# The modulation vector's sum: DVE's multiply-adds replaced by ACT's scaling and an adding transfer

## The chip, the cores and the metric

The kernel runs on one core of one Trainium2 chip. The metric is the device time of one execution in microseconds: the median of three runs is 1697.87 us (1697.62 to 1698.13). TensorE does the matrix products, ACT (ScalarE) and DVE (VectorE) the elementwise work, GpSimd (POOL) little beside issuing some transfers, and SP issues nearly all loads. All transfers run on 16 DMA engines.

## The reference

Two transformer layers, one after the other, on x of 1 x 256 x 2048 in float32. The first is a norm, a mix of three kinds of attention, a projection, and a wide layer of squared-ReLU units, then a norm. The second one is modulated by a vector c of 2048 numbers. Only this part matters here:

```
mod = silu(c) @ w_ada + b_ada                 # w_ada: 2048 x 6144
shift, scale, gate = split(mod, 3)
h = rmsnorm(x, pre_g) * (1 + scale) + shift   # then the second layer's products with h
...
return x + gate * rmsnorm(o, post_g)
```

silu(c) @ w_ada is a product of one row with 48 MiB of weights.

## The kernel before

Weights are float32 and are multiplied as a high and a low part. A *chunk* is one load of weights, mostly 1 MiB (128 partitions x 2048 columns) into one of four `raw` buffers (pool `rawp`, `NRAW = 4`). Its two halves of 1024 columns are split one by one: ACT writes the high part (L402), DVE subtracts it from the raw half to get the low part (L403). The parts go to one of six pairs of split tiles (`NSPLIT = 6`), and TensorE multiplies them with the activations (L265, L266 for products with features on the partitions; L297 to L299 for those with tokens).

`run` (L360) walks over the chunks in program order. For each half chunk it issues the loads up to four chunks ahead (`do_dma`), the splits up to four halves ahead (`do_split`), and the half's products; then `pump` (L345) lets each of the side generators take one step. A generator that yields n skips n steps. `drain` (L350) runs a generator to its end at once. After the first eight half chunks the order of instructions on each engine is set by a scheduler, which goes by program order as priority and by its own estimate of when operands are there, and which hands out the buffers of a pool; on the chip each engine then works through its queue in order, and SP and GpSimd do so with the transfers that they issue.

The modulation is such a generator, `ada_gen` (L1033). It is spawned after the first four half chunks of the wide layer. For each of three thirds (shift, scale, gate) it goes through 16 row blocks k: it loads 128 rows x 2048 columns of `w_ada` (1 MiB) into a buffer `rawa` of the same pool of four (L1042), and DVE adds it, times silu(c) of the row on each partition, to the accumulator `acc` (L1044 for the first block, L1046 for the others). Each block yields 3, so there is one in four half chunks. After 16 blocks `acc` is cut into high and low parts (L503, L504), and TensorE sums over the partitions (L1090).

The wide layer has eight slices of 16 half chunks with `w_mlp_in` and 16 with `w_mlp_out`. Before the last 16 half chunks with `w_mlp_out`, `load_gf` (L1009) drains `ada_gen` and has GpSimd read the scale row `G` from DRAM and the gain `gf`; DVE multiplies with both after each of the last products (L982, L985). That is 237 steps of `ada_gen` after its first. The gate's sums are taken in the last of these chunks, and the second layer's input is put together after them (`h3_gen`, L1136).

Of the kernel before, what the change touches and what calls it, by code (L numbers as in the profile page):

```python
# [13 lines left out]
ALU = mybir.AluOpType  # L14
# [16 lines left out]
class Chunk:  # L31
    """One load of weights: raw f32 columns, cut into nh pieces of high and low parts (hw columns each).
    Without a load, mm only uses what earlier chunks left. in_heap: the parts go to two general tiles each."""

# [9 lines left out]
class Joined:  # L44
    """Two tiles of 512 columns in place of one of 1024; a slice lies in one of them."""

# [10 lines left out]
def kernel(  # L57
# [23 lines left out]
    def table(name, after):  # L81
        """Switch the activation tables right after one of the engine's instructions."""
        with tc.issue_after(after.ins):
            return act.preload_act_table_set(name)
# [19 lines left out]
    def split_cols(dst, src, w=256):  # L104
        """dst[:, :w] and dst[:, w:2w] become the high and the low part of src."""
        act.activation(dst[:, 0:w], src, AF.Copy)
        ve.tensor_tensor(dst[:, w:2 * w], src, dst[:, 0:w], op=ALU.subtract)
# [3 lines left out]
    def rsqrt(dst, src, scale, tmp):  # L111
        """dst = (src * scale + EPS) ** -0.5 refined by one Newton step; tmp: two scratch views."""
        v, t = tmp
        ve.tensor_scalar(v, src, scale, EPS, op0=ALU.mult, op1=ALU.add)
        act.activation(dst, v, AF.Ln)
        act.activation(dst, dst, AF.Exp, scale=-0.5)
        ve.tensor_tensor(t, v, dst, op=ALU.mult)
        ve.tensor_tensor(t, t, dst, op=ALU.mult)
        ve.tensor_scalar(t, t, -0.5, 1.5, op0=ALU.mult, op1=ALU.add)
        return ve.tensor_tensor(dst, dst, t, op=ALU.mult)  # L120
# [3 lines left out]

# [1 line left out]
    wi = w_in[0].rearrange("(k p) n -> p k n", p=P)  # L126
# [16 lines left out]

    # the tensor engine's clock rises while it is busy: products that nothing reads, until the input is there
    def warm_up(n):
# [9 lines left out]

# [1 line left out]
    csq = H("csq")  # L157
# [47 lines left out]
    def setup_gen():  # L205
# [9 lines left out]
        yield 0  # L215
        # relative-position biases as vectors over distance, kept in DRAM for skewed reads
        for nh, c0, w, o_, bd in ((12, 0, 384, oh, bd1), (8, 12, 512, oh2, bd2)):
# [7 lines left out]
    def bias_tile(src, w, h0, hstep, joff, name):  # L225
        """[query, 2 heads, 256 keys] out of a per-distance vector."""
        b = H(name)
        base = src[:, :]
        po.dma_start(v2(b), bass.AP(tensor=base.tensor, offset=base.offset + h0 * w + joff,
                                    ap=[[1, P], [hstep * w, 2], [1, 256]]))  # L230
        return v2(b)[:, :, ::-1]

# [1 line left out]
    def W(ap):  # L234
        return ap.rearrange("(k p) n -> p k n", p=P)

    def modeA(src, c0, acts, evac, kt=KT, seg=None, need=None, name="a", k_row0=0, nh=2):
        """256 output features on partitions: psum [128, n, 512] = W.T @ [hi | lo]."""
        st = {}
# [37 lines left out]
    def modeB(dmas, acts, evac, ncols=512, kts=(4, 4, 4, 4), need=None, name="b", by_t=False):  # L277
        """tokens on partitions: psum [128, t, ncols] = act.T @ W. by_t: the first token block over the
        whole contraction, then the second; evac(ps, t) after each."""
        st = {"parts": {}}  # L280
# [149 lines left out]

# [1 line left out]
    h1 = [H(f"h1_{k}", F32R) for k in range(KT)]  # L432

    def x_transposes(src, dst, gain, name, kks):
        """dst[k] = split(gain * src.T) for the k-tiles kks (pairs)."""
        for k in kks:
# [15 lines left out]
    def sumsq(dst, src, name, scale=1.0):  # L452
        """dst [128,1] = sum of squares of scale * src [128, <=512]."""
        sc = H(f"sq_{name}")
        last["sq"] = act.activation(sc[:, 0:src.shape[-1]], src, AF.Square, scale=scale, accum_out=dst)

    def row_of(col, dst, name):
        """dst [128, 128]: every partition holds the token values of col [128, 1]."""
        pr = PA(f"pr_{name}")
        dg = H(f"dg_{name}")  # L460
        ve.tensor_scalar(dg[:, 0:128], ident, col, None, op0=ALU.mult)
        te.matmul(pr[:, 0:P], ones, dg[:, 0:128], start=True, stop=True)
        return ve.tensor_copy(dst, pr[:, 0:P])
# [22 lines left out]
    def evac_sum(ps, name, row=None):  # L486
        """[128, 2, 256] = the two halves of a feature-on-partition product, times a token row."""
        o = H(name)
# [11 lines left out]
    def in_parts(o, name):  # L500
        """o as high and low part."""
        hi, lo = H(f"{name}h", F32R), H(f"{name}l", F32R)
        act.activation(hi, o, AF.Copy)  # L503
        ve.tensor_tensor(lo, o, hi, op=ALU.subtract)  # L504
        return hi, lo
# [20 lines left out]

# [1 line left out]
    def ones_row_norm(tiles, width, name):  # L528
        """rstd row [128, 256] over the features of tiles ([128, 2, 256] each)."""
        parts = []  # L530
# [90 lines left out]

# [1 line left out]
    def softmax(segs, nsk, sk, n, name):  # L623
        """segs: [128, keys] logits, normalised in place; nsk, sk: [128, n] sink values, negated and plain."""
        nm, den, es = S(f"nm{name}", n), S(f"den{name}", n), S(f"es{name}", n)
# [14 lines left out]
    def swa_bias(h):  # L640
        """[query, keys of the second block, then of the first] for one head."""
        b = H("swab")
# [58 lines left out]

# [1 line left out]
    def gla_gen():  # L703
        QD, KI, OB = {}, {}, {}
        st = {}
        # gates
        pbl = PA("pbl")
# [193 lines left out]

# [1 line left out]
    wo = w_out[0]  # L903
    # contraction tiles: 0-5 sliding window (heads i and i+6), 6-9 stick-breaking, 10-15 gated
    def wo_dma(c0):
# [45 lines left out]

# [1 line left out]
    r2sq = C([P, 2], "r2sq")  # L953
# [65 lines left out]

    # modulation: silu(c) @ w_ada as multiply-adds, then one sum over partitions  # L1020
    wa = W(w_ada_2[0])
# [3 lines left out]
    gp = [None] * 4  # L1025
    # sel[:, n, m] = (n == m): sums over partitions, put into row n
    sel = C([P, 4, 4], "sel")
# [5 lines left out]
    def ada_gen():  # L1033
# [4 lines left out]
        for third in range(3):  # L1038
            acc = big.tile([P, D], F32, name="acc", tag="acc")
            for k in range(KT):  # L1040
                raw = rawp.tile([P, 2048], F32, name="rawa", tag="raw")
                sy.dma_start(raw, wa[:, k, third * D:(third + 1) * D])  # L1042
                if k == 0:
                    ve.tensor_scalar(acc, raw, e[:, 0:1], None, op0=ALU.mult)  # L1044
                else:
                    ve.scalar_tensor_tensor(out=acc, in0=raw, scalar=e[:, k:k + 1], in1=acc,  # L1046
                                            op0=ALU.mult, op1=ALU.add)
                yield 3
            parts = []
# [27 lines left out]
    def ada_row(r, third):  # L1077
        """(1 + scale) * pre_norm_g or gate * post_norm_g, into DRAM for reads by all partitions."""
        bg, pg_ = H("bada"), H("pada_g")
# [51 lines left out]

# [1 line left out]
    h3 = [H(f"h3_{k}", F32R) for k in range(KT)]  # L1133
    r3 = C([P, 2], "r3")

    def h3_gen(t):  # L1136
        for n in range(4):
            drain(recs["fin", n, t])
        u, r12 = S("u", 1), S("r12", 1)
        # (mean(y^2) / (mean(x^2) + EPS) + EPS) * (mean(x^2) + EPS), y = x * norm_final  # L1140
        ve.tensor_reduce(u, ss3[:, t, :], axis=AX.X, op=ALU.add)
# [26 lines left out]
    def make_xn():  # L1168
        with tc.issue_after(last["sum"].ins):
            # mean(x^2) + EPS out of the sum of squares scaled by EPS / D  # L1170
            ve.tensor_reduce(r3, ss3[:, :, 0:4], axis=AX.X, op=ALU.add)
# [31 lines left out]

# [1 line left out]
    def att_gen():  # L1205
# [118 lines left out]

    # grouped linear map of the pooling branch
    wpg = w_pool_group_2[0].rearrange("g (k p) d -> p (g k) d", p=P)
# [30 lines left out]

# [1 line left out]
    wm, wba, wbp = W(w_merge_2[0]), W(w_branch_attn_2[0]), W(w_branch_pool_2[0])  # L1359
# [37 lines left out]

# [1 line left out]
    wo2 = W(w_out_2[0])  # L1399
# [68 lines left out]
def _constants():  # L1468
    """Arrays that depend on shapes alone: identity, triangles, bucket one-hots, window counts."""
    import numpy as np  # L1470
# [56 lines left out]
```

## Time and profile before

| | |
|---|---|
| time, median of 3 runs | 1697.87 us (1697.62 to 1698.13) |
| profiled execution, from its first to its last instruction (span) | 1695.6 us |
| what lies around the span, against the median | 2.3 us |
| TensorE busy | 1681.5 us, 99% |
| DVE / ACT / GpSimd busy | 1154.3 / 860.6 / 56.7 us |
| DVE, multiply-adds of the modulation | 45 of 2349 ns |
| loads of the modulation | 48 of 1 MiB, first issued at 380.8 us, last at 967.8 us |
| transfers, whole span | 363.87 MB, mean 215 GB/s |

The profiled execution has no time of its own beside its span; the runs are timed without a profile. Busy times are shares of one engine's time; several engines work beside each other, so they do not add up to the span. The chain of waits follows the work back from the last instruction, and what lies on it set the end. A wait of an engine is its idle time before an instruction, put down to what came last.

### The profile page before, as it was taken

The page shows a single profiled execution, that of the slowest core. Times are in us where ns is not written, and L with a number is a line of the kernel's source. Part 1 is how long each engine was busy: PE and PEld are TensorE (multiplying, and loading weights), DVE is VectorE, ACT ScalarE, POOL GpSimd, SP SyncE. Part 2 cuts the span into 40 slices and gives each one's busy share as a digit, 9 for nine tenths or more (in the row PEclk, how much of TensorE's full clock was granted, in tenths as well). Part 3 has the DMA queues.
Part 4 walks back from the last instruction along what each step waited for, and adds up shares of the span by engine and source line. Part 5 has one row for each costly group of instructions (what it writes and reads, how often), then busy time and mean ns, then how long its engine had stood idle before and what let it go on. Part 6 is the DMA issues. An engine that isn't in the chain of part 4 may idle for free.

```text
span 1695.6 us, 23129 instructions
## 1 busy us (share of the span) xinstructions
PE 1681.5 (99%) x9085; PEld 1446.3 (85%) x9085; DVE 1154.3 (68%) x1437; ACT 860.6 (51%) x1278; POOL 56.7 (3%) x113
## 2 busy tenths in 40 slices
PE   9999999999999999999999999999999999999998
PEld 7888899888888888888888888788888888888887
DVE  6566767557787668777778775877775655555554
ACT  6455657445444444444444354665455544554442
POOL 2002100000000000000000010010100000000000
PEclk9999999999999999999999999999999999999999
DMA  9645646757888678877788876555645655565652
GB/s 322 190 138 139 153 140 172 199 188 264 283 296 280 219 246 292 281 282 238 277 279 288 285 245 214 172 188 180 194 156 167 215 184 189 184 188 185 214 188 71
DMA packets 265405, 363.87 MB, mean 215 GB/s; under 512 B 9809, under 2 KB 206063, under 8 KB 259152
## 3 DMA queue, kind: packets, MB, share of 16 engines
q1 hardware_dynamic: 261472, 353.53, 63.6%
q0 software_dynamic: 3792, 8.86, 2.6%
q8 instruction: 71, 1.16, 0.3%
q14 instruction: 38, 0.31, 0.1%
q10 hardware_dynamic: 32, 0.01, 0.0%
HBM read 360.20 MB, written 2.15 MB: 214 GB/s over the span
## 4 chain that ended last, share of the span: by engine, by line
PE 95%; DVE 2%; ACT 1%; DMA 1%; issue 0%; SPq 0%; DVEq 0%
PE ps_w L265 14%; PE ps_w L266 7%; PE ps_m L265 7%; PE ps_w L297 7%; PE ps_w L299 7%; PE ps_w L298 7%; PE ps_m L266 4%; PE ps_b L265 4%; PE ps_wo L299 3%; PE ps_wo L297 3%; PE ps_wo L298 3%; PE ps_b L266 2%; PE ps_gp L265 2%; PE ps_ga L265 2%; PE ps_u L265 2%; PE ps_q L265 2%
## 5 line engine op out<-in xcount | busy, mean ns | idle before, releaser
L402 ACT ACTIVATE hi<-raw 128x1024 fp32r<-128x1024 f32 (+3 forms) x570 | 588.1, 1034 | 733.4 <-PE ps_w L299 169.5
L403 DVE TENSOR_TENSOR lo<-raw,hi 128x1024 fp32r<-128x1024 f32 (+3 forms) x570 | 675.2, 1190 | 411.7 <-ACT hi L402 407.7
L265 PE MATMUL ps_w<-h,hi 128*128 128x512 f32 x1024 | 359.6, 397 | 0.0
L266 PE MATMUL ps_w<-h,lo 128*128 128x256 f32 x1024 | 286.1, 279 | 0.0
L265 PEld LDWEIGHTS ps_w<-h,hi 128*128 128x128 f32 x1024 | 192.2, 188 | 46.3
L297 PE MATMUL ps_w<-hi,sl 128*128 128x512 f32 x512 | 199.4, 389 | 0.0
L299 PE MATMUL ps_w<-hi,sl 128*128 128x512 f32 x512 | 199.3, 389 | 0.0
L298 PE MATMUL ps_w<-lo,sl 128*128 128x512 f32 x512 | 199.2, 389 | 0.0
L266 PEld LDWEIGHTS ps_w<-h,lo 128*128 128x128 f32 x1024 | 193.0, 188 | 0.3
L265 PE MATMUL ps_m<-h,hi 128*128 128x512 f32 x512 | 181.3, 399 | 0.0
L266 PE MATMUL ps_m<-h,lo 128*128 128x256 f32 x512 | 143.8, 281 | 0.0
L1046 DVE SCALAR_TENSOR_TENSOR acc<-rawa,silu_c,acc 128x2048 f32<-128x2048 f32 x45 | 105.7, 2349 | 30.3 <-DMA rawa<-in_w_ada_dram 30.1
L265 PEld LDWEIGHTS ps_m<-h,hi 128*128 128x128 f32 x512 | 96.2, 188 | 23.9
L299 PEld LDWEIGHTS ps_w<-hi,sl 128*128 128x128 f32 x512 | 96.1, 188 | 20.2
L297 PEld LDWEIGHTS ps_w<-hi,sl 128*128 128x128 f32 x512 | 96.1, 188 | 20.1
L298 PEld LDWEIGHTS ps_w<-lo,sl 128*128 128x128 f32 x512 | 96.1, 188 | 19.8
L266 PEld LDWEIGHTS ps_m<-h,lo 128*128 128x128 f32 x512 | 96.7, 189 | 0.0
L297 PE MATMUL ps_wo<-hi,mg 128*128 128x512 f32 (+1 forms) x160 | 55.5, 347 | 0.0
L299 PE MATMUL ps_wo<-hi,mg 128*128 128x512 f32 (+1 forms) x160 | 55.5, 347 | 0.0
L298 PE MATMUL ps_wo<-lo,mg 128*128 128x512 f32 (+1 forms) x160 | 55.5, 347 | 0.0
L995 DVE SCALAR_TENSOR_TENSOR xt<-ps_w,r2sq,xt 128x512 f32<-128x512 f32 x64 | 45.1, 745 | 8.1 <-PE ps_w L299 8.1
L265 PE MATMUL ps_b<-ya,hi 128*128 128x512 f32 x128 | 45.6, 399 | 0.0
(517 smaller groups left out, 2766.9 us busy)
## 6 DMA issues: line engine op xcount, KB each, us to landing
raw<-in_w_mlp_in_dram SPq DMA_DIRECT2D x64, 1024.0 KB, 5.6
raw<-in_w_mlp_out_dram SPq DMA_DIRECT2D x64, 1024.0 KB, 5.2
raw<-in_w_in_dram SPq DMA_DIRECT2D x48, 1024.0 KB, 5.0
rawa<-in_w_ada_dram SPq DMA_DIRECT2D x48, 1024.0 KB, 5.4
raw<-in_w_merge_dram SPq DMA_DIRECT2D x32, 1024.0 KB, 5.3
raw<-in_w_out_dram SPq DMA_DIRECT2D x20, 1024.0 KB, 5.1
raw<-in_w_in_dram SPq DMA_DIRECT2D x24, 768.0 KB, 4.5
raw<-in_w_in_dram SPq DMA_DIRECT2D x20, 512.0 KB, 5.2
```

Of the source, the lines that this page charges most:

```text
L265: te.matmul(ps[:, n, :], hi[:, s], a, start=(k == 0), stop=False)
L266: te.matmul(ps[:, n, 0:256], lo[:, s], a[:, 0:256], start=False, stop=(k == kt - 1))
L297: te.matmul(o, ah, hi[:, s], start=(k == 0), stop=False)
L298: te.matmul(o, ah, lo[:, s], start=False, stop=False)
L299: te.matmul(o, al, hi[:, s], start=False, stop=(k == ktot - 1))
L402: act.activation(hi[:, 0:c.hw], r, AF.Copy)
L403: ve.tensor_tensor(lo[:, 0:c.hw], r, hi[:, 0:c.hw], op=ALU.subtract)
L995: ve.scalar_tensor_tensor(out=d, in0=ps[:, t if isinstance(ts, tuple) else 0, :], scalar=r2sq[:, t:t + 1], in1=d, op0=ALU.mult, op1=ALU.add)
L1046: ve.scalar_tensor_tensor(out=acc, in0=raw, scalar=e[:, k:k + 1], in1=acc, op0=ALU.mult, op1=ALU.add)
```

## The change

In each block k, ACT now multiplies the two halves of the loaded buffer by silu(c), in two steps of the generator. In the first block of a third it writes to `acc`, in the others back into the buffer. Then, in the next step and except for the first block, a transfer that GpSimd issues adds the whole buffer to `acc` in place. DVE's instructions on L1044 and L1046 are gone. A block now takes a step for each half and one for the transfer, after which two are skipped. Comments and docstrings are gone as well.

```diff
             for k in range(KT):
                 raw = rawp.tile([P, 2048], F32, name="rawa", tag="raw")
                 sy.dma_start(raw, wa[:, k, third * D:(third + 1) * D])
-                if k == 0:
-                    ve.tensor_scalar(acc, raw, e[:, 0:1], None, op0=ALU.mult)
-                else:
-                    ve.scalar_tensor_tensor(out=acc, in0=raw, scalar=e[:, k:k + 1], in1=acc,
-                                            op0=ALU.mult, op1=ALU.add)
-                yield 3
+                dst = raw if k else acc
+                for i in range(2):
+                    half = slice(i * 1024, (i + 1) * 1024)
+                    act.activation(dst[:, half], raw[:, half], AF.Copy, scale=e[:, k:k + 1])
+                    yield 0
+                if k:
+                    po.dma_start(acc, raw, accum_op=ALU.add)
+                yield 2
             parts = []
```

## Rows read from the trace of the kernel before

**Rows 1.** Page: busy time of each engine (share, instructions), chain by engine.
```profile
PE 1681.5 (99%) x9085; PEld 1446.3 (85%) x9085; DVE 1154.3 (68%) x1437; ACT 860.6 (51%) x1278; POOL 56.7 (3%) x113
...
PE 95%; DVE 2%; ACT 1%; DMA 1%; issue 0%; SPq 0%; DVEq 0%
```

**Rows 2.** Windows: stretch and length, busy per engine, PEclk, DMA share, GB/s.
```profile
607.00:614.00 7.00, 7.00 (x40) 5.84 (x39) 4.26 (x6) 2.51 (x3) 0.00 (x0) 1.00 1.08 369
634.00:638.00 4.00, 4.00 (x25) 3.51 (x24) 3.96 (x6) 1.88 (x4) 0.00 (x0) 1.00 1.06 424
10.00:30.00 20.00, 18.81 (x111) 15.97 (x110) 14.67 (x25) 14.41 (x29) 3.79 (x14) 1.00 1.09 335
380.00:973.00 593.00, 593.00 (x3040) 503.05 (x3039) 454.34 (x442) 265.03 (x315) 4.03 (x8) 1.00 0.79 272
```

**Rows 3.** Waits of TensorE, whole span: total us, times, longest; the largest one.
```profile
PE pt_h L441 <- DMA xt<-in_x_dram: 1.8, 3, 0.9
```

**Rows 4.** Waits between 380 and 973 us, ACT's largest.
```profile
ACT hi L402 <- PE ps_w L265: 137.7, 86, 2.0
ACT hi L402 <- PE ps_w L299: 136.1, 85, 2.2
```

**Rows 5.** Waits of SP's queue between 380 and 973 us.
```profile
SPq L250 <- DVE lo L403: 148.1, 34, 5.6
...
SPq L250 <- DVE acc L1046: 52.5, 22, 2.4
SPq L1006 <- DVE acc L1046: 48.0, 21, 2.4
```

**Rows 6.** Instructions on rawa: ns min/median/max, first and last start; waits; landing.
```profile
L1042 SPq DMA_DIRECT2D rawa<-in_w_ada_dram x48: 340/341/341, 380.8 to 967.8; - x48
L1046 DVE SCALAR_TENSOR_TENSOR acc<-rawa,silu_c,acc x45: 2339/2351/2354, 399.4 to 972.7; 128x2048 f32<-128x2048 f32 x45
L1044 DVE TENSOR_SCALAR acc<-rawa,silu_c x3: 1281/1281/1281, 386.2 to 804.0; 128x2048 f32<-128x2048 f32 x3
...
  DMA rawa<-in_w_ada_dram: 30.1, 33
...
DMA to landing us min/median/max: 4.8/5.4/7.5
```

**Rows 7.** Groups by line, 380 to 973 us: count, busy us, mean ns, idle before.
```profile
L403 DVE TENSOR_TENSOR lo<-raw,hi 128x1024 fp32r<-128x1024 f32 x213 | 258.3, 1222 | 103.2 <-ACT hi L402 102.9
...
L402 ACT ACTIVATE hi<-raw 128x1024 fp32r<-128x1024 f32 x213 | 226.1, 1061 | 321.4 <-PE ps_w L265 137.7 <-PE ps_w L299 136.1 <-issue 40.1
```

**Rows 8.** Order of time, GpSimd: start, us, instruction.
```profile
1004.73 0.56 POOL L1014 DMA_DIRECT2D G<-gdr  x1
```

**Rows 9.** Page: DMA queues of SP and of GpSimd: packets, MB, share.
```profile
q1 hardware_dynamic: 261472, 353.53, 63.6%
q0 software_dynamic: 3792, 8.86, 2.6%
```

**Rows 10.** DMA issues by line: count, size of each, median us to landing.
```profile
raw<-in_w_mlp_in_dram SPq DMA_DIRECT2D x64, 1024.0 KB, 5.6
...
rawa<-in_w_ada_dram SPq DMA_DIRECT2D x48, 1024.0 KB, 5.4
...
G<-gdr POOLq DMA_DIRECT2D x4, 256.0 KB, 8.8
...
gp<-gdr POOLq DMA_DIRECT2D x4, 256.0 KB, 5.3
```

**Rows 11.** Order of time, SP: one modulation load's issue.
```profile
644.23 0.34 SPq L1042 DMA_DIRECT2D rawa<-in_w_ada_dram  x1
```

**Rows 12.** Order of time, DVE: the multiply-add of that load.
```profile
649.86 2.35 DVE L1046 SCALAR_TENSOR_TENSOR acc<-rawa,silu_c,acc 128x2048 f32<-128x2048 f32 x1 [0.59 <-DMA rawa<-in_w_ada_dram]
```

**Rows 13.** Order of time, DVE: the first products with gf and G.
```profile
1066.02 0.69 DVE L982 TENSOR_TENSOR xt<-xt,gf 128x512 f32<-128x512 f32 x1
1066.74 0.69 DVE L985 TENSOR_TENSOR Z<-xt,G 128x512 f32<-128x512 f32 x1
```

## The prediction

> **What bounds the kernel now.** I read the page first: TensorE is busy for 1681.5 of 1695.6 us, and the chain that ended last is 95% TensorE [rows 1]. Then the stretch in which the modulation runs, 380 to 973 us, in the view by windows: TensorE is busy in 593.00 of 593 us at the full granted clock (1.00), DVE in 454, ACT in 265, and the 16 DMA engines show a mean share of 0.79 at 272 GB/s [rows 2]. So nothing that DVE is relieved of can shorten this stretch; it can only stay or grow. The largest of TensorE's waits in the whole span is 1.8 us, for the input at the start [rows 3]: it never waits for weights here. What protects it is seen in the other waits: ACT's splits wait 137.7 + 136.1 us for TensorE to give a pair of split tiles back, so the splits run six half chunks ahead [rows 4]; and the load queue (SP) waits for a raw buffer to be given back, mostly by DVE's second half of the split, and for 48.0 and 52.5 us by the modulation's multiply-add [rows 5]. The four raw buffers are thus always claimed, with some spare time in each.
>
> **The pace.** The first modulation load starts at 380.8, the last of 48 at 967.8 us [rows 6]; by the code's counts they lie 209 half chunks of products apart (3 x 15 x 4 within the thirds, 17 and 12 between them), so a half takes 587.0 / 209 = 2.81 us. A piece is now due every 4 halves (11.2 us). In the new code a piece costs a step for the first half of the scaling, one for the second, one for the transfer and two skipped: 5 halves, 14.0 us.
>
> **Part by part.**
> 1. DVE loses 45 multiply-adds of 2349 ns and 3 first products of 1281 ns, 105.7 + 3.8 = 109.5 us [rows 6]. TensorE does not wait for DVE in this stretch, so it is worth 0.
> 2. ACT gains 96 activations of 128x1024. The nearest row is the split's first half, same tile shape, 1061 ns [rows 7]: 102 us in all, 2.1 per piece. ACT is busy 265/593 = 45% of the stretch, 6.3 of 14.0 us; with 2.1 more it has 5.6 us idle per piece. Hidden, as long as a scaling does not wait for its load by more than that; DVE's multiply-add waited 30.1 us over 33 cases [rows 6].
> 3. GpSimd gains 45 transfers. Issuing one takes it 0.56 us [rows 8], 25 us in all on an engine with 56.7 us of work [rows 1]: hidden.
> 4. The transfers themselves are the cost. They are 1 MiB each, tile to tile, with an add. The trace of before has no such transfer. Both queues are counted against the same 16 engines [rows 9], and GpSimd's four reads of G landed after a median of 8.8 us beside the weight stream, the same size of gp in 5.3 us with the stream thinner [rows 10]; so I let the new transfers share the engines with the loads. In 14.0 us these must bring 2.5 MiB of weights and 1 MiB of modulation. Rate of the loads: the longest dense stretch that I found beside the modulation gave 369 GB/s for 7 us, a short one 424 for 4 us, and the start 335 for 20 us [rows 2]. At 369 a MiB takes 1.0486 MB / 369 = 2.84 us, so 3.5 take 9.9 us and 4.1 are left. Lower bound of an add: it is charged as one pass over 1 MiB at the best rate, 2.47 us, and fits. Upper bound: it has to fetch both operands, 2 MiB, at 335 GB/s: 6.3 us. I take two operands at 424 GB/s, since its rows are 8 KB long in each partition as those of rawa: 4.9 us. Sum 9.95 + 4.95 = 14.9 against 14.0: 0.9 us over per piece, 36 us for the 40 transfers that are paced (6). With everything at 369 it is 15.6 (1.6 over), at 335 it is 17.2 (3.2 over).
> The Trainium skill has a rule on this price ("Collectives: The Full Stack", The bandwidth ceiling: the fold count and why AG ≠ RS ≠ AR): an add in the transfer engines issues two source reads, and the reduction ran at 32.35 GB/s where the plain copy ran at 62.28. By it the sum is that of two operands; no run here shows it yet.
> 5. Raw buffers. A piece holds its buffer from its issue at 644.23 to the end of the multiply-add at 652.21 us, 8.0 us [rows 11, 12]. Afterwards: landing 5.4 [rows 6], scaling 1.06, the next step 2.8 later, then the transfer, 5 to 11 us (one or two landings of 5.4): 14 to 21. A weight chunk needs at least 5.6 (landing) + 2.8 (the next half) + 1.06 + 1.22 (its split) = 10.7 us [rows 7, 10]. Per 14.0 us there are 4 x 14.0 = 56 buffer-us; 2.5 x 10.7 + 21 = 48. It fits until a transfer takes 19 us, but the spare time that hid late loads is mostly gone.
> 6. What is left over. The draining before the last eight output chunks comes 237 steps after the start. At 5 instead of 4 steps the modulation's last load would come at step 256 and its end at 264, so there 4 loads and 5 transfers are still to come: 40 of the 45 transfers are paced, 5 come in a heap. The heap is 4 x 2.84 + 5 x 4.9 = 36 us of transfer work, beside 8 MiB of weights (23 us), in 16 halves, 45 us: 14 us over. At 0 it would be spread into the gaps that the output products leave; at 36 nothing of it would be beside them. G, which GpSimd issued from 1004.7 us on with gf, DVE first used right after gf at 1066.0 [rows 8, 13]; both now stand behind these transfers on GpSimd's queue, which it works through in order. The cover is 61 us less a landing of 9; where the heap uses it up, the eight pairs of products with gf and G (0.69 + 0.69 us each) fall together at the end: up to 11 us more.
> Sum: 40 x 0.9 + 14 = 50 us over the stretch. The profiled execution spans 1695.6 us; the runs' median of 1697.87 is 2.3 more, which I leave as it is. 1697.9 + 50 = 1748 us. Time that TensorE has lost here does not come back, for it is the bound before and after it.
>
> **Rivals.**
> (a) The add is charged as one pass. Then 9.9 + 2.5 = 12.4 of 14.0 us, the heap is 4 x 2.84 + 5 x 2.47 + 23 = 47 of 45 us, and the time is 1698 to 1701, not slower. It is decided by whether a transfer takes under 4.1 us of the engines. For it: the mean of 272 GB/s leaves room below the 369. Against it: the room is there because no buffer was free (5), and this gets tighter.
> (b) The chain on the accumulator. Each transfer waits on GpSimd for the one before, since both change acc; behind it GpSimd has only the next ones, and the buffer it holds stops SP, which issues in order, so the weights wait too. It decides from 14.0 - 0.5 = 13.5 us per transfer on: at 18 us it costs 4.5 x 40 = 180, and with the heap 1892 us. For it: 256 KB of G took 8.8 us from GpSimd [rows 10], which times four is 35. Against it: two landings of 1 MiB are 10.8 us.
> (c) ACT becomes the late one. A scaling at the head of ACT's queue holds the splits behind it, and DVE behind these. If landings double to 10.8 us, a scaling waits some 5.4 + 2.1 = 7.5 us, 1.9 over ACT's idle 5.6: 40 x 1.9 = 76, and with the heap 1788 us. Against it: six half chunks of split weights, 16.9 us, stand between ACT and TensorE, so that a single late load is not felt.
> (d) Faster. TensorE's idle time outside the stretch is 1695.6 - 1681.5 = 14 us; a lucky new order around the second block's input at 1096 us could take a few of them: 1693. Nothing in the change aims there.
>
> **How the numbers follow.** My forecast with its own range of 1715 to 1800: 0.47. (a) 0.18, (b) 0.17, (c) 0.12, (d) 0.06. Below 0.2% (3.4 us) a measurement of this kernel can't tell a change. Faster is (d), 0.06; the same is (a), 0.18; slower is the rest, 0.76. The range takes in (a) and (c) and (b) up to a transfer of 17 us, 1695 to 1870.
>
> **What would show it.** TensorE's busy share in the modulation's stretch below 100%, with idle before products that waits put down to the splits, and these to loads or scalings that wait for rawa; DMA share near 1 there; acc transfers landing after 8 to 12 us; SP waiting on these transfers; the stretch longer by some 36 us, the rest between 1050 and 1130. Wrong, if TensorE is still full in it (then the add is cheap, (a)), if a transfer lands later than 13.5 us (b), or if the loss lies outside both stretches.

## The result and the profile after

The changed kernel takes 1854.28 us (median of 4 runs, 1850.64 to 1857.43) against 1697.89 us before: a ratio of 1.0921, interval 1.0907 to 1.0935. It is slower by 156 us, inside the range and on the side that was forecast, but three times the forecast loss of 50.

The page of the changed kernel: busy time of each engine, and the queues of SP (q1) and GpSimd (q0).
```profile
PE 1726.5 (93%) x9085; PEld 1469.7 (79%) x9085; DVE 1040.5 (56%) x1389; ACT 943.8 (51%) x1374; POOL 96.4 (5%) x158
...
q1 hardware_dynamic: 261472, 353.53, 57.6%
q0 software_dynamic: 10272, 56.05, 16.1%
```
Against [rows 1] the 9085 products take 45.0 us longer, and TensorE is idle for 1851.2 - 1726.5 = 124.7 us where it was for 14.1: 45.0 + 110.6 = 155.6 us, all of the loss. DVE's relief, 114 us, bought nothing.

Windows of the changed kernel (columns as in [rows 2]): from the first modulation load to where the kernel before had its last product with the MLP's first matrix (1008 us), from there to that product here (1095), and the output chunks behind it.
```profile
380.00:1008.00 628.00, 574.59 (x2836) 479.43 (x2836) 318.17 (x366) 303.18 (x363) 31.11 (x39) 0.96 0.91 273
1008.00:1095.00 87.00, 82.79 (x407) 69.24 (x406) 41.29 (x46) 42.56 (x50) 5.19 (x6) 0.96 0.94 282
1095.00:1235.00 140.00, 99.54 (x384) 77.39 (x384) 54.31 (x61) 52.60 (x62) 11.87 (x17) 0.85 0.93 269
```
TensorE was full at a granted clock of 1.00 in 593 of 593 us [rows 2]. Now it is idle for 53 us of the first stretch, 4 of the second and 40 of the third, and between such stalls it is granted 0.96 and 0.85 of its 2.4 GHz, in the mean. Parts of these stretches run at 1.2 GHz: some of the products with the MLP's first matrix take 796 ns where the median is 395. The engines of the DMA are busier, 0.91 to 0.94 in place of 0.79, yet they move no more: 273 GB/s in place of 272. The splits themselves take no longer beside the transfers: between 380 and 1008 us ACT's take 1.05 us and DVE's 1.22, against 1.06 and 1.22 [rows 7].

The products with the MLP's first matrix (ns min/median/max, first and last start):
```profile
L265 PE MATMUL ps_w<-h,hi x1024: 387/395/796, 383.9 to 1095.0; 128*128 128x512 f32 x171
```

DMA issues of the changed kernel: count, size, median us to landing.
```profile
raw<-in_w_mlp_in_dram SPq DMA_DIRECT2D x64, 1024.0 KB, 8.6
raw<-in_w_mlp_out_dram SPq DMA_DIRECT2D x64, 1024.0 KB, 7.8
...
rawa<-in_w_ada_dram SPq DMA_DIRECT2D x48, 1024.0 KB, 5.5
acc<-rawa POOLq DMA_DIRECT2D x45, 1024.0 KB, 8.2
```
The adding transfer lands after 8.2 us, the weights after 8.6 where it was 5.6 [rows 10]. The modulation's loads keep their 5.5: they start only when a transfer has ended, as the next two views show.

Waits of the changed kernel, whole span (total us, times, longest), first of the engines, then of SP's queue.
```profile
DVE lo L403 <- ACT hi L402: 649.9, 309, 22.1
...
ACT rawa L1046 <- DMA rawa<-in_w_ada_dram: 325.6, 43, 15.3
...
PE ps_w L297 <- ACT hi L402: 34.3, 10, 17.8
...
PE pt_z L1159 <- DVE Z L1156: 14.0, 1, 14.0
```
```profile
SPq L1042 <- DMA acc<-rawa: 199.3, 36, 13.5
...
SPq L1006 <- DMA acc<-rawa: 43.8, 4, 12.5
...
SPq L250 <- DMA acc<-rawa: 26.0, 4, 11.8
```
36 of the 48 modulation loads wait on SP for the transfer before them, since they were given its buffer; 269 us of SP's time goes this way, where DVE's multiply-add cost 100 [rows 5].

One such turn in order of time (start, us, engine).
```profile
487.07 0.34 SPq L1042 DMA_DIRECT2D rawa<-in_w_ada_dram  x1
...
493.50 2.19 ACT L1046 ACTIVATE rawa<-rawa,silu_c 128x1024 f32<-128x1024 f32 x2 [9.00 <-DMA rawa<-in_w_ada_dram]
...
495.98 0.86 POOL L1049 DMA_DIRECT2D acc<-rawa  x1 [16.16 <-ACT rawa L1046]
...
503.90 0.34 SPq L1042 DMA_DIRECT2D rawa<-in_w_ada_dram  x1
```
Load 6.4 us, scaling 2.5, transfer 7.9, and only then the next load: 16.8 us, where a piece is due every 14.0. That looked like the cause. By the engines' time it comes to the same: q1 takes 0.576 x 1851.2 us for 353.53 MB, 3.16 us of the 16 engines' time per MiB, and the transfers add (0.161 x 1851.2 - 0.026 x 1695.6) / 45 = 5.64 us each; 3.5 x 3.16 + 5.64 = 16.7 us per piece. The modulation's loads are in fact issued 16.8 us apart (the median). Two theories with one number: the experiments had to part them.

### The profile page after: what moved, and what is told of

Read it like the earlier page. It is cut to its first block, busy times and chain, and to the rows that moved or that the text cites. A ratio compares the mean times of both kernels' runs of the same rounds, so it can differ in the third digit from the quotient of the medians.

```text
span 1851.2 us, 23271 instructions
## 1 busy us (share of the span) xinstructions
PE 1726.5 (93%) x9085; PEld 1469.7 (79%) x9085; DVE 1040.5 (56%) x1389; ACT 943.8 (51%) x1374; POOL 96.4 (5%) x158
## 3 DMA queue, kind: packets, MB, share of 16 engines
q1 hardware_dynamic: 261472, 353.53, 57.6%
q0 software_dynamic: 10272, 56.05, 16.1%
## 5 line engine op out<-in xcount | busy, mean ns | idle before, releaser
L403 DVE TENSOR_TENSOR lo<-raw,hi 128x1024 fp32r<-128x1024 f32 (+3 forms) x570 | 668.1, 1189 | 653.5 <-ACT hi L402 649.9
L402 ACT ACTIVATE hi<-raw 128x1024 fp32r<-128x1024 f32 (+3 forms) x570 | 573.1, 1027 | 440.4 <-PE ps_wo L299 74.2
L265 PE MATMUL ps_w<-h,hi 128*128 128x512 f32 x1024 | 375.0, 409 | 36.6 <-DVE mlp L491 17.2
L266 PE MATMUL ps_w<-h,lo 128*128 128x256 f32 x1024 | 293.5, 287 | 5.0 <-DVE lo L403 5.0
L265 PEld LDWEIGHTS ps_w<-h,hi 128*128 128x128 f32 x1024 | 199.4, 195 | 88.1 <-ACT hi L402 22.5
L1046 ACT ACTIVATE rawa<-rawa,silu_c 128x1024 f32<-128x1024 f32 x90 | 99.3, 1143 | 325.6 <-DMA rawa<-in_w_ada_dram 325.6
L297 PE MATMUL ps_w<-hi,sl 128*128 128x512 f32 x512 | 206.9, 404 | 48.0 <-ACT hi L402 34.3
L266 PEld LDWEIGHTS ps_w<-h,lo 128*128 128x128 f32 x1024 | 200.3, 196 | 8.0 <-DVE lo L403 7.8
L299 PE MATMUL ps_w<-hi,sl 128*128 128x512 f32 x512 | 204.4, 399 | 0.0
L1049 POOL DMA_DIRECT2D acc<-rawa x45 | 39.2, 872 | 878.1 <-ACT rawa L1046 790.3
L265 PE MATMUL ps_u<-h,hi 128*128 128x512 f32 x128 | 45.6, 399 | 0.0
```

The costliest lines, as they stand in the source:

```text
L265: te.matmul(ps[:, n, :], hi[:, s], a, start=(k == 0), stop=False)
L266: te.matmul(ps[:, n, 0:256], lo[:, s], a[:, 0:256], start=False, stop=(k == kt - 1))
L297: te.matmul(o, ah, hi[:, s], start=(k == 0), stop=False)
L299: te.matmul(o, al, hi[:, s], start=False, stop=(k == ktot - 1))
L402: act.activation(hi[:, 0:c.hw], r, AF.Copy)
L403: ve.tensor_tensor(lo[:, 0:c.hw], r, hi[:, 0:c.hw], op=ALU.subtract)
```

## The experiments

LOOP: the buffer that goes load, scaling, transfer, load sets the pace. ENGINES: the transfer takes so much of the shared 16 engines that all loads land late, whoever waits for it. Diffs are against the changed kernel unless said; times are medians of 4 runs, beside 1698.0 to 1698.7 for the kernel before.

**e1_accacc.** acc is added to itself, so the scaled pieces are not summed; a buffer is free after its scaling.
```
- po.dma_start(acc, raw, accum_op=ALU.add)
+ po.dma_start(acc, acc, accum_op=ALU.add)
```


> The transfer adds acc to itself instead of the scaled piece (the sum is left out; bytes, add and chain on acc stay). A piece's buffer is free right after its scaling. LOOP (load 6.4 + scaling 2.5 + transfer 7.9 = 16.8 us run one after the other, since the next piece's load takes the buffer that the transfer holds): the loop falls to 9 us, SP no longer waits for transfers, the loss goes to under 40 us: 1700 to 1735 us, granted clock at least 0.99. ENGINES (loads are late since the 16 engines are full): the same bytes, so most of the loss stays: 1800 to 1855 us, weights land at a median of 8 us or more and ACT waits for them.


1826.63 us, 1.0757 (1.0741 to 1.0773). Not a clean test: with nothing to hold them the transfers ran ahead, back to back, some 11.4 us apart, and were through at 1129 us in place of 1205. e5 repeats it at pace.

**e2_plain.** The same order of instructions, the transfer a copy: the addition is left out.
```
- po.dma_start(acc, raw, accum_op=ALU.add)
+ po.dma_start(acc, raw)
```


> The transfer copies the scaled piece onto acc without an add (the sum is left out). It prices the add. LOOP: with a copy landing in t us the period is 8.9 + t; at t = 5.4 that is 14.3, 0.3 over the 14.0 that a piece has: some 12 us in the paced part, in all 1710 to 1760 us. ENGINES: one pass in place of two, 12.4 of 14.0 us: 1700 to 1750 us. If the add costs nothing, the copy lands at 8 us and the time stays at 1850 us.


1764.65 us, 1.0391 (1.0374 to 1.0407). The page of this kernel, the queue of GpSimd and the landing of the copies:
```profile
q0 software_dynamic: 10272, 56.05, 9.5%
...
acc<-rawa POOLq DMA_DIRECT2D x45, 1024.0 KB, 5.2
```
A copy takes (0.095 x 1761.0 - 44.1) / 45 = 2.74 us of the engines, the addition 5.64: 2.06 times as much, and 89.6 us of the 156. The Trainium skill gives the two source reads of an add as the reason ("Collectives: The Full Stack", The bandwidth ceiling: the fold count and why AG ≠ RS ≠ AR), with 62.28 to 32.35 GB/s, a ratio of 1.93, among four ranks. The trace agrees in the ratio; the second read itself it does not show, for the queue counts the same 10272 packets and 56.05 MB for both.

**e3_noheap.** The last five pieces are left out, those that the forecast saw in a heap.
```
- for k in range(KT):
+ for k in range(KT if third < 2 else 11):
```


> The last five blocks of the third third are left out (part of the gate's sum), so nothing is left for the draining. LOOP: the paced part keeps its loss, 40 x 2.5 = 100 us: 1785 to 1805 us; the heap and the late G were the other 50. If instead most of the loss was the heap: 1740 us or less. ENGINES gives the same as LOOP here.


1802.28 us, 1.0608 (1.0592 to 1.0624). The heap is worth 52 us, not 14, and the paced part 1802.28 - 1698.69 = 104, not 36. Both terms were too small.

**e4_own2.** The pieces get two buffers of their own; NSPLIT goes from 6 to 4 to make room.
```
- NSPLIT = 6
+ NSPLIT = 4
  ...
+ modp = ctx.enter_context(tc.tile_pool(name="modp", bufs=2))
  ...
- raw = rawp.tile([P, 2048], F32, name="rawa", tag="raw")
+ raw = modp.tile([P, 2048], F32, name="rawa", tag="rawa")
```


> The modulation's pieces get a pool of two buffers of their own; the room comes from two of the six split pairs. LOOP: a load waits for the transfer before the last, so the loop has 2 x 14.0 us for 16.8 and the weights keep four buffers: the paced loss goes, some of the heap stays: 1700 to 1740 us. ENGINES: the bytes are the same, the loss stays or grows with more loads in flight: 1800 us or more. SPLITS (four pairs in place of six are too few): stalls at the splits without late loads, some tens of us, which a control without the change would show too.


1905.66 us, 1.1232 (1.1211 to 1.1252): slower. Again not clean, since the loads were put in another order and the transfers ran back to back, some 13 us apart. e6 holds each piece's load in its place.

**e5_accpaced.** e1 at pace: each transfer stands behind a GpSimd copy of two columns of its scaled piece (the pieces are not summed).
```
- po.dma_start(acc, raw, accum_op=ALU.add)
+ seen = po.tensor_copy(S("seen", 2), raw[:, 1023:2048:1024])
+ with tc.issue_after(seen.ins):
+     po.dma_start(acc, acc, accum_op=ALU.add)
```


> As e1 (the transfer adds acc to itself, the sum is left out), but each transfer stands behind a GpSimd copy of two columns of its scaled piece, so that transfers keep the pieces' pace; the buffer is free after that copy. The order of loads is that of the changed kernel. LOOP (load, scaling and transfer in series through one buffer): no longer a loop, the paced part loses under 15 us, the heap its 50 or less: 1705 to 1755 us. ENGINES (3.5 loads of 3.16 us and an add of 5.6 us of all 16 engines, by the queues' shares 16.7 us per piece): same bytes, same 16.7 us: the paced part still loses about 100 us, 1800 to 1855 us.


1924.15 us, 1.1329 (1.1312 to 1.1346). The page's DMA issues in this kernel:
```profile
raw<-in_w_mlp_in_dram SPq DMA_DIRECT2D x64, 1024.0 KB, 8.7
raw<-in_w_mlp_out_dram SPq DMA_DIRECT2D x64, 1024.0 KB, 9.7
...
rawa<-in_w_ada_dram SPq DMA_DIRECT2D x48, 1024.0 KB, 11.8
acc<-acc POOLq DMA_DIRECT2D x45, 1024.0 KB, 12.6
```
No load waits for a transfer any more, and the kernel loses 70 us more than the changed one. Load and transfer now run side by side, and both land after 12 us in place of 5.5 and 8.2. LOOP's 1705 to 1755 is far off, but ENGINES (1800 to 1855) missed too: transfers are some 19 us apart, where by the engines' time a piece asks for 3.5 x 3.16 + (0.141 x 1923.0 - 44.1) / 45 = 16.1, and the mean DMA share between 700 and 930 us is only 0.84. And the run changes one thing more: the weight loads that are now given a piece's buffer wait 307 us on SP (40 times) for that piece to land. e6 has no such wait.

**e6_own2paced.** e4 with each piece's load held behind the load that was issued last ahead of it on SP (sy.last).
```
+ with tc.issue_after(sy.last.ins):
      sy.dma_start(raw, wa[:, k, third * D:(third + 1) * D])
```


> As e4 (two buffers of their own for the modulation's pieces, four split pairs), and each modulation load stands on SP behind the last weight load before it in the program, so that there are again 2 or 3 weight loads to a piece. LOOP: a load waits for the transfer before the last: no paced loss, 1705 to 1755 us. ENGINES: transfers about 16.5 us apart in the paced part, 1800 to 1870 us. If four split pairs matter by themselves, more, with waits for TensorE at the splits.


1911.73 us, 1.1257 (1.124 to 1.1273); transfers land after 12.1 us, pieces after 12.6, weights after 10.1. The same picture as e5 with buffers of their own, and above ENGINES' 1800 to 1870: here loads wait 51 us in all for transfers (4 times) and none for a piece's landing. So LOOP is not needed for the loss; in the changed kernel it keeps load and transfer apart. What four split pairs cost by themselves no run shows.

**e7_noscale.** ACT scales only the first piece of each third; the sum is then of unscaled pieces.
```
+ if k == 0:
      act.activation(dst[:, half], raw[:, half], AF.Copy, scale=e[:, k:k + 1])
```


> ACT does not scale the pieces after the first of a third (the scaling is left out); the transfer adds each piece as it was loaded. LOOP: 6.4 + 7.9 = 14.3 us against 14.0, paced loss 12 us or less: 1705 to 1760 us. ACT (the scalings at the head of ACT's queue hold up the splits): likewise. ENGINES: same bytes, most of the loss stays: 1800 us or more, with splits waiting for loads of weights in place of scalings.


1900.33 us, 1.12 (1.1177 to 1.1222). That is as ENGINES said and against both others: taking 2.3 us of ACT work and its wait out of the turn makes it slower. Transfers land after 9.9 us. Here too the buffers go round another way: 387 us of SP's 431 for transfers are weight loads that were given a piece's buffer, 70 of 269 in the changed kernel.

**e8_actdve.** ACT scales as in the change, DVE adds, no transfer.
```
- po.dma_start(acc, raw, accum_op=ALU.add)
+ ve.tensor_tensor(acc, acc, raw, op=ALU.add)
```


> ACT's scaling alone: DVE adds the scaled piece to acc by a tensor_tensor, no transfer is issued; the new pace stays, and the heap with it. All theories: no loss in the paced part (1.00 busy TensorE), so 1697 to 1702 us if the heap's 50 us are its transfers'; 1710 to 1730 us if the heap costs by its loads alone. ACT by itself: if ACT's scaling is what costs, 1750 us or more.


1711.59 us, 1.0081 (1.0064 to 1.0097). One stretch of it by windows:
```profile
700.00:930.00 230.00, 228.00 (x1167) 193.28 (x1166) 163.93 (x167) 128.01 (x152) 1.53 (x3) 0.99 0.75 257
```
TensorE is as good as full. The scaling on ACT and the slower pace cost 13 us together; the other 143 come with the transfer in place of DVE's addition.

**e9_lone_add.** The transfer by itself: the kernel before (DVE multiplies and adds), at five half loads per piece, NSPLIT 5 to make room for a spare tile, which is added to itself once per piece.
```
  (against the kernel before)
- NSPLIT = 6
+ NSPLIT = 5
  ...
+ extra = big.tile([P, D], F32, name="extra", tag="extra")
+ po.memset(extra, 0.0)
  ...
+ if k:
+     po.tensor_copy(extra[:, 0:2], acc[:, 0:2])
+     po.dma_start(extra, extra, accum_op=ALU.add)
- yield 3
+ yield 4
```


> DVE keeps its multiply-adds as before, at the changed kernel's pace of five half loads per piece; beside each piece GpSimd issues a transfer that adds a spare 1 MiB tile to itself, which nothing waits for but the next such transfer; NSPLIT is 5, to make room for the tile. ENGINES (an adding transfer takes some 5.6 us of the 16 engines and lengthens every load beside it, whoever waits for it): the five halves ask for 3.5 x 3.16 + 5.6 = 16.7 us where TensorE gives 14.0, so 45 pieces lose about 90 to 120 us without any wait for the transfer: 1790 to 1830, weight landings 7 to 9 us, granted clock under 0.98. WAITS (the loss is the buffer held until the transfer ends, and the scaling in ACT's queue): neither is here, so within 1% of the same kernel with copies: 1700 to 1725.


1876.89 us, 1.1063 (1.1036 to 1.109).

**e10_lone_copy** has the spare tile copied onto itself, all else the same.
```
- po.dma_start(extra, extra, accum_op=ALU.add)
+ po.dma_start(extra, extra)
```


> The kernel e9_lone_add with each transfer a plain copy of the spare tile onto itself, the same bytes written and the same order of instructions on every engine. ENGINES: 3.5 x 3.16 + 2.7 = 13.8 us per piece, just under the 14.0 that TensorE gives: 1700 to 1730, copies landing in about 5 us, weights in 6 to 7. WAITS: the same, 1700 to 1725. The difference between e9_lone_add and this is the price of the addition with no one waiting: ENGINES 80 to 120 us, WAITS under 15.


1789.3 us, 1.0544 (1.0526 to 1.0561), where both theories had 1730 or less.

**e12_lone_tiny** (16 columns) and **e13_lone_half** (1024) cut e9's transfer; the order of loads and products stays that of e9. The edit of e12 (in e13 `0:1024` stands in both places):
```
- po.dma_start(extra, extra, accum_op=ALU.add)
+ po.dma_start(extra[:, 0:16], extra[:, 0:16], accum_op=ALU.add)
```


> The kernel e9_lone_add with each extra transfer cut to 16 of 2048 columns (8 KB): the same 45 issues, the same order of loads and products, next to no bytes. It is the base of e9_lone_add and e10_lone_copy. ENGINES (the loss is the time that the extra transfer takes of the 16 engines): 1700 to 1715, so that the copy of e10_lone_copy has cost 75 to 90 us and the addition of e9_lone_add 160 to 180. PACE (five half loads per piece, NSPLIT 5 and the issues from GpSimd make the loss, not the bytes): 1750 to 1790.

> The kernel e9_lone_add with each extra transfer cut to 1024 of 2048 columns (512 KB added). ENGINES, in proportion: half an addition takes 2.8 us of the 16 engines, as a whole copy does (2.7), so the time is that of e10_lone_copy: 1775 to 1805. EXCESS (only what goes over TensorE's 14.0 us per piece is lost; 3.5 x 3.16 + 2.8 = 13.9): 1700 to 1720. PRESENCE (a transfer of the other queue slows the loads beside it whatever its size): 1840 to 1880.


e12: 1708.68 us, 1.006 (1.0045 to 1.0075); e13: 1775.13 us, 1.0455 (1.0437 to 1.0472). The pages of the four, e12, e13, e10, e9: GpSimd's queue, the first weights, the pieces, the extra transfer (not for e12, whose transfers are 8 KB).
```profile
q0 software_dynamic: 10272, 9.23, 3.1%
...
raw<-in_w_mlp_in_dram SPq DMA_DIRECT2D x64, 1024.0 KB, 5.7
...
rawa<-in_w_ada_dram SPq DMA_DIRECT2D x48, 1024.0 KB, 4.9
```
```profile
q0 software_dynamic: 10272, 32.45, 9.1%
...
raw<-in_w_mlp_in_dram SPq DMA_DIRECT2D x64, 1024.0 KB, 7.1
...
rawa<-in_w_ada_dram SPq DMA_DIRECT2D x48, 1024.0 KB, 8.4
...
extra<-extra POOLq DMA_DIRECT2D x45, 512.0 KB, 9.0
```
```profile
q0 software_dynamic: 10272, 56.05, 8.7%
...
raw<-in_w_mlp_in_dram SPq DMA_DIRECT2D x64, 1024.0 KB, 7.7
...
rawa<-in_w_ada_dram SPq DMA_DIRECT2D x48, 1024.0 KB, 8.6
extra<-extra POOLq DMA_DIRECT2D x45, 1024.0 KB, 9.2
```
```profile
q0 software_dynamic: 10272, 56.05, 14.6%
...
raw<-in_w_mlp_in_dram SPq DMA_DIRECT2D x64, 1024.0 KB, 9.8
...
rawa<-in_w_ada_dram SPq DMA_DIRECT2D x48, 1024.0 KB, 10.8
extra<-extra POOLq DMA_DIRECT2D x45, 1024.0 KB, 11.7
```
Each share times its span (1706.3, 1773.0, 1785.5, 1873.1), less e12's 52.9 us, over 45, is the engine time of an extra transfer over that of e12's 8 KB; the time over e12 is its price:

| | engine us each | loss, us | loss per engine us |
|---|---|---|---|
| half an addition (e13) | 2.41 | 66 | 0.61 |
| a copy (e10) | 2.28 | 81 | 0.79 |
| an addition (e9) | 4.90 | 168 | 0.76 |

With the 44.1 us of the kernel before taken off, as was done for the changed kernel, the three are 2.61, 2.47 and 5.10 us.

Nothing but the next such transfer waits for these, and no buffer is held by them; still the addition costs 168 us. That is ENGINES, and more than it said (1790 to 1830). e13 falls on the lower edge of ENGINES in proportion and refutes both others: a transfer's mere presence would have cost as much as e9, the excess over 14.0 us alone next to nothing. e12, at 1.006, is as ENGINES said: the pace, the five split pairs and the issues from GpSimd cost 10 us together.

In e10 one stretch by windows shows what a copy that should have fitted (3.5 x 3.2 + 2.5 = 13.7 of 14.0 us) does:
```profile
700.00:930.00 230.00, 214.95 (x1037) 178.13 (x1036) 149.79 (x146) 86.94 (x102) 18.49 (x30) 0.98 0.86 300
```
TensorE is idle for 15 of 230 us though the engines' mean share is 0.86. A mean share under 1 is no proof of room.

**e11_poolscale.** GpSimd scales in place of ACT, just ahead of its transfer; the order of the loads is unchanged.
```
- act.activation(dst[:, half], raw[:, half], AF.Copy, scale=e[:, k:k + 1])
+ po.tensor_scalar(dst[:, half], raw[:, half], e[:, k:k + 1], None, op0=ALU.mult)
```


> The changed kernel with the scaling of each piece on GpSimd, just ahead of its transfer, in place of ACT; the order of the loads is unchanged. ENGINES: the transfers and loads ask for the same, so 1830 to 1870, and PE's waits for ACT's high parts turn into ones for the loads themselves. ACTQUEUE (a late piece at the head of ACT's queue holds up the splits of weights that have landed, 7.2 us per piece): that wait goes from ACT to GpSimd, where nothing but the transfer is behind it, and the time falls by half the loss or more, to 1700 to 1780.


2003.75 us, 1.1801 (1.1783 to 1.1818), which no theory had. Its chain of waits, one piece after another:
```profile
581.14 7.00 DMA acc<-rawa
588.19 4.84 DMA rawa<-in_w_ada_dram
593.20 5.68 POOL rawa L1046 x2
599.16 7.10 DMA acc<-rawa
...
606.77 7.11 DMA rawa<-in_w_ada_dram
614.16 3.49 issue
617.66 2.86 POOL rawa L1046
620.80 6.96 DMA acc<-rawa
```
Here the loop does decide. GpSimd takes 3.09 us per half where ACT took 1.14; a turn becomes 18 to 22 us, longer than the engines need, whose share is down to 0.76 between 700 and 930 us. So a turn that is long enough does set the pace; in the changed kernel it is just as long as the sum of the engines' time. As a test of ACT's queue the run says nothing.

**e14_late, e15_lone_copy_late.** The piece is used two half loads later: the scaling in the changed kernel, the multiply-add in e10. The order of the loads is unchanged.
```
  (e14)
  dst = raw if k else acc
+ yield 1
  ...
- yield 2
+ yield 0

  (e15, against e10)
  sy.dma_start(raw, ...)
+ yield 1
  ...
- yield 4
+ yield 2
```


> The changed kernel with each piece's scaling two half loads later: the load is issued as before, ACT's two scalings and the transfer come at the third and fourth of the five steps; the order of the loads is unchanged. HEAD (what turns late landings into stalls is the wait of a scaling at the head of ACT's queue, 7.2 us per piece): that wait falls under 2 us per piece and the time by 40 us or more, to 1760 to 1815, though transfers start later. HOLD (what counts is how long a piece keeps its buffer, and with it the next load): it is kept some 5.6 us longer, 45 times, and the time rises to 1870 to 1990, with SP waiting longer for acc's transfers. ENGINES alone: no change, 1840 to 1865.

> The kernel e10_lone_copy with DVE's multiply-add of each piece two half loads later; nothing waits for the extra copy here either. HEAD (DVE's multiply-add waited 204.4 us for late pieces, 4.5 per piece, ahead of the splits behind it): that wait goes, and of the 81 us over e12_lone_tiny half or more with it: 1710 to 1750. HOLD (buffers are what is short): 1800 to 1870. ENGINES alone: 1780 to 1800.


e14: 1900.16 us, 1.1197 (1.1178 to 1.1216). Its waits on SP's queue:
```profile
SPq L1042 <- DMA acc<-rawa: 221.0, 29, 13.4
...
SPq L1006 <- DMA acc<-rawa: 70.4, 8, 12.5
SPq L250 <- DMA acc<-rawa: 60.0, 7, 12.0
```
SP waits 351 us for transfers in place of 269, and 46 us are lost, as HOLD said; in this family a buffer kept longer counts. e15: 1786.11 us, 1.0517 (1.0501 to 1.0533), 3 us from e10, as ENGINES alone said. The group of DVE's multiply-add in it:
```profile
L1049 DVE SCALAR_TENSOR_TENSOR acc<-rawa,silu_c,acc 128x2048 f32<-128x2048 f32 x45 | 105.8, 2351 | 211.4 <-DMA rawa<-in_w_ada_dram 200.5
```
DVE waited 204.4 us for pieces in e10 and still waits 200.5: used later, the piece also comes later. HEAD, that the wait at the head of a queue is what costs, is not borne out, but the wait was not taken away either. One step that the traces show is on SP: in e10 the weight loads that are given a piece's buffer wait for that piece to land, 188 us in 38 cases (e9: 264, e13: 172, e12: 6).
```profile
SPq L250 <- DMA rawa<-in_w_ada_dram: 101.5, 19, 7.5
...
SPq L1006 <- DMA rawa<-in_w_ada_dram: 86.3, 19, 6.2
```
No run takes this wait away without another change, and e6 is slow without it; so by what step a late landing becomes TensorE's stall stays open.

## Why the prediction was wrong

**Steps 1 to 3 held.** DVE's relief is worth nothing; e8 hides the scaling on ACT but for a part of its 13 us; GpSimd's issue (0.87 us, not 0.56) is hidden.

**Step 4 failed; it is the cause of the wrong size.** The mechanism is the one forecast, a transfer at the price of two operands on engines that the loads share, but "0.9 us over per piece, 36 us" measured 104 (e3). The addition was mis-sized by 0.7 us a piece: 4.95 forecast, 5.64 measured in the changed kernel (5.10 in e9). The loads were mis-sized by 0.7 to 1.3: 2.84 us per MiB came from 369 GB/s over 7 us, a row in which the engines' share is 1.08 [rows 2]; as engine time that is 3.07. The whole stretch, 0.79 at 272 GB/s [rows 2], gives 3.05, and [rows 9] give 0.636 x 1695.6 us for 353.53 MB, 3.2, over the whole span. With 3.05 to 3.2 and 5.64 a piece asks for 16.3 to 16.8 us, 2.3 to 2.8 over 14.0, times 40: 93 to 113 us, around the 104. The rows stood there; a dense moment's rate was taken as the price.

The rule beneath it failed too. It charged only what goes over TensorE's 14.0 us. e10 and e13 ask for less and lose 81 and 66 us; e9 and e5 ask for 16.2 and 16.1 us and go at some 17 and 19. That the corrected sum meets the changed kernel's 16.8 is thus in part luck. Where the loop keeps transfer and load apart, as in e2, the rule does better: there the copy costs 53 us over e8, and TensorE's idle time is mostly that of the draining, 36 us between 1090 and 1210 us.

**Step 5 failed in its reading.** "It fits until a transfer takes 19 us": a transfer lands after 8.2, and SP waits 269 us. The count of buffer-us was a mean; it did not ask which load is next given the piece's buffer. Here it is mostly the next piece (36 of 48); in e5 and e7 it is weight loads, and both are slower. Freeing the buffer gained nothing (e5, e6), and load and transfer then landed later; keeping it longer costs 46 us (e14). What the 269 us of SP's wait are worth by themselves no run shows.

**Step 6: 14 us forecast, 52 measured.** The heap of transfers came, with G issued at 1206 us in place of 1004.7 [rows 8] and the products with gf and G after it. With 3.2 and 5.64 us the same working gives 4 x 3.2 + 5 x 5.64 + 8 x 3.2 = 67 of 45 us, 22 over. Two more terms are seen in this stretch: TensorE waits 14.0 us for Z at its end, which the step had priced at "up to 11 us more" and left out of the sum, and its clock is 0.85. How the 52 divide among them no run shows.

**What was in no step** is the granted clock: the same 9085 products take 45 us longer, of 156. Long stalls are paid for again in the products around them: from 1170 to 1200 us, where TensorE is busy for 9 of 30 us, the granted clock is 0.61, then 0.71. Short ones need not be: between 1095 and 1110 us it is idle for 3.3 us in all and keeps 1.00.

**Rivals.** (a), one pass, falls: 2.06 times a copy. (b) asked for transfers of 13.5 us and more; they land after 8.2, and a turn that sets the pace is seen only in e11. (c) saw the scaling's wait: 325.6 us over 43 cases, 7.6 each, is what it forecast (7.5). But e7, without scalings, is slower, and e8, with them and no transfer, loses 13 us; so no run shows the wait by itself to be what costs.

**The signs.** Most that the prediction named came: TensorE idle behind splits, DMA share up to 0.94, transfers after 8.2 us, SP waiting for them. The sizes did not: the paced part lost 104 us and not 36, and with that the rest came not between 1050 and 1130 us but from 1095 to 1235.

No version here beats the kernel before; of those that scale on ACT, e8 comes nearest.

## What to carry to other kernels

An adding transfer between tiles is work for the engines that bring the weights, twice that of a copy; before work goes from a half idle engine to the DMA, put its engine time beside that of the loads, at the mean price of the stretch and not at the best rate seen. Here, with four load buffers, much of that time was lost even at mean shares of 0.83 to 0.91: 0.6 to 0.8 us per us of engine time (e9, e10, e13), 0.4 to 0.6 where the loop kept transfer and load apart (e2 and the changed kernel, over e8). The clock that long stalls take is in these figures. A serial turn that is as long as the loss asks for need not be its cause: take it away once before believing it.

## What the runs showed of the hardware

- 1 MiB from tile to tile takes 2.5 to 2.7 us of the 16 engines as a copy and 5.1 to 5.6 with an addition; it lands after 5.2 and 8.2 us apart from the pieces' loads (e2, changed kernel), 9.2 and 11.7 beside them (e10, e9).
- 8 KB transfers of the same count (e12) leave the loads' landing about where it was: 5.7 and 4.9 us, against 5.6 and 5.4 [rows 10].
- GpSimd's multiplication by a column took 3.09 us for 128x1024 in f32, ACT's 1.14.
